# The merge's row statistics among the constants: the left side of SBUF 128 bytes higher

## The chip, the cores and the metric

The kernel runs on one core of a Trainium2 chip. Five engines share the work: TensorE (PE) multiplies matrices, VectorE (DVE) and ScalarE (ACT) do elementwise work and empty the accumulators, GpSimd (POOL) does elementwise work in SBUF, and SyncE (SP) issues most transfers. SBUF is the on-chip memory of 128 partitions; an address below is a byte within a partition. The metric is the device time of one launch in microseconds. The kernel before took 2745.03 us, the median of three runs from 2735.61 to 2746.83.

## The reference

One layer of an encoder on 2048 tokens of 1024 features, all in float32. With S = 2048 and D = 1024:

```
h  = RMSNorm(x)
z  = h @ W_in                  # (S, D) @ (D, 4352): q, k, v of two attentions, two gates
yA = windowed GQA, 8 heads, |t-s| <= 128, ALiBi and a sink logit
yB = 2-D neighbourhood attention, 8 heads, 32 x 64 grid, learned position bias
x  = x + (sigmoid(gate_A) * (yA @ Wp_A) + sigmoid(gate_B) * (yB @ Wp_B)) @ W_out
x  = x + relu(RMSNorm(x) @ W_up)^2 @ W_down      # hidden width 4096
out = RMSNorm(x)
```

## The kernel before

**Precision.** A float32 operand is split into a high and a low part in the reduced format `fp32r`; a product is three matmuls: high by high, high by low, low by high (`mm3`, lines 193 to 195, and `mm3s`, lines 239 to 241). In `PE.matmul(ps, lh, rh)` the second argument is loaded into the array as weights and the third moves through it, 512 columns at a time in most places. The result adds up in a PSUM bank.

**Stages**, in the order of time:

1. Input projection (0 to 376 us). Two of the four token blocks are multiplied by W_in with a Strassen-like scheme (`in_quad`): seven products, numbered in the order 1, 2, 5, 6, 7, 4, 3, each of 24 matmuls, or 12 where one output of 128 columns is made. The weights are `zwhl`; what moves are pages `zh1` to `zh7`. Pages 1, 2, 6, 7 and 4 lie on the left side of SBUF, pages 5 and 3 on the right.
2. Attention A (376 to 709 us) and attention B (709 to 1088 us, its last pieces to 1103). Between the attention's short matmuls stand those of a filler: the other two blocks times W_in (`feature_tile`), where `hT` moves and `whl` are the weights. In attention A `ph` and `pl` move in the product with the values, and `ka` in the scores; in attention B `phb`, `plb` and `kb`.
3. Merge (1088 to 1506 us), four token blocks. For each, eight feature tiles are made from `page` (moving) and `whl` (weights), gated, and split into `mh` and `ml`. Then four row tiles `xr` are made by 24 matmuls per bank with `mh` or `ml` as weights and `wo` moving; x is added. `rstd_of` (line 210 on) makes the row statistics: ScalarE sums the squares into `st`, VectorE adds (L218), GpSimd takes the power (L219), VectorE scales the rows (L225). The rows are turned, scaled into `h2s`, and written out.
4. Up projection (1506 to 2117 us, begun at 1447), with `ubh` moving and `uwhla`, `uwhlb` as weights, and the same seven products.
5. Down projection and the last norm (2117 to 2737 us), with `dwh` moving and `dah` as weights.

**Order of work.** Instructions stand on each engine's queue in an order that a planner writes out ahead of time. It plays the program through with estimated costs and keeps to the dependences; so the merge's `page` and `wo` matmuls, for one, are interleaved on PE. At run time each engine keeps that order and waits on semaphores.

**Memory.** Tiles come from pools. A pool with `side="left"` is stacked upward from the low end of SBUF, a pool on the right downward from the high end. The pool `cp`, opened first on the left, holds the constants and stays until the end. Sizes are rounded up to 32 bytes. Ahead of the first wide tile lie 1024 bytes for the transfers' descriptors, four framework constants of 32 bytes, and `cp`: `ident` 512, `g_mix` 32, `g_mlp` 32, `bg` 64, `sink_t` 32, `power` 32, `warm` 32. That makes 1888 = 3*512 + 352. The right side counts down from 229344 = 447*512 + 480. Wide tiles have multiples of 512 bytes, so that left tiles begin at 352 modulo 512 and right tiles at 480. There is one place on the left that differs: in the merge `mh` and `ml` are opened after `st`, whose four buffers have 32 bytes each, and so they lie 128 bytes higher, at 480. The up and down stages have all their tiles on the right.

A new tile over the place of old ones waits for their last use (`reuse_waits`), tile by tile. `T(pl, shape, dt, tag, bufs)` takes a pool, or the pool of that tag where `pl` is a dictionary; `bufs` tiles of one tag form a ring.

The pools of the merge on the left are opened in lines 922 to 925, in this order: `pwo` (for `wo`), `ph2` (for `h2s`), and the dictionary `p4x`.

Of the kernel before, what the change touches and what calls it, by code (L numbers as in the profile page):

```python
# [92 lines left out]
def encoder_layer(ctx, tc, x, norm_mix, w_in, b_gate, sink, rpb, w_pa, w_pb, w_out,  # L93
# [4 lines left out]
    def pool(name, side=None, space=None, stack=None):  # L98
        kw = {"reuse_waits": "tile"} if space is not DRAM else {}
        if side:  # L100
            kw["side"] = side
        if space:
            kw["space"] = space
        return (stack or ctx).enter_context(tc.tile_pool(name=name, bufs=1, **kw))

    def pools(stack, side, tags, name):

        return {t: pool(f"{name}_{t}", side=side, stack=stack) for t in tags}

    cp = pool("cp", side="left")  # L110
# [11 lines left out]
    def T(pl, shape, dt, tag, bufs):  # L122
        n_t[0] += 1
        pl = pl[tag] if isinstance(pl, dict) else pl
        return pl.tile(shape, dt, tag=tag, bufs=bufs, name=f"{tag}_{n_t[0]}")
# [796 lines left out]
    s_wo = ExitStack()  # L922
    pwo = pool("pwo", side="left", stack=s_wo)
    ph2 = pool("ph2", side="left", stack=s_wo)
    p4x = pools(s_wo, "left", ("xr", "junk", "st", "mh", "ml"), "m")
    wo = []

    def load_wo(n):
# [216 lines left out]
    for b in range(NB):  # L1145
        yh, yl = first_y if b == 0 else load_y(b)
        mh = T(p4x, [P, KC, BT], F32R, "mh", 1)
        ml = T(p4x, [P, KC, BT], F32R, "ml", 1)
# [261 lines left out]
```

## Time and profile before

| | |
|---|---|
| median of three runs | 2745.03 us |
| lowest, highest | 2735.61, 2746.83 us |
| the profiled execution | 2739.11 us |
| its span in the profile | 2737.3 us |
| mean granted TensorE clock | 0.989 |
| matmuls | 12332 |
| data moved by DMA | 480.86 MB, 176 GB/s on average |

In the rows that follow, PE is TensorE's matmul and PEld its weight load; "x" is a count. A group's row has line, engine, operation, tiles (written <- read), shape and count, then its busy time in us and the mean duration of one in ns, and last the idle time of the engine ahead of it and what ended that. A matmul's duration overlaps the next one's start; what a stream of matmuls costs is the spacing from start to start, which a window's length over its count gives where the engine has no idle time. "Granted clock" is the share of TensorE's full clock.

### The profile page before, as it was taken

The numbers are of one execution on the slowest core, as the hardware profiler recorded it, in microseconds if no ns is written. First come the engines' busy times: TensorE is split into PE (matmuls) and PEld (weight loads), VectorE is DVE, ScalarE is ACT, GpSimd is POOL, SyncE is SP. The second block draws the span as 40 slices with busy tenths as digits, with TensorE's granted clock in tenths as the row PEclk, the third lists the DMA queues.
The fourth block names the chain that finished last, engine by engine and source line by source line (L and its number), as shares of the span: only waits on it lengthen the run. The fifth ranks groups of instructions, "written<-read, shape, count | busy, mean of one in ns | idle before, by whom it ended". The sixth has DMA issues, their size and how long they took to land. (4 is left out here: it accounts for less than half of the span.)

```text
span 2737.3 us, 35101 instructions
## 1 busy us (share of the span) xinstructions
PE 2654.3 (97%) x12332; PEld 2185.1 (80%) x12332; DVE 1558.6 (57%) x2352; ACT 1248.0 (46%) x2225; POOL 843.0 (31%) x671
## 2 busy tenths in 40 slices
PE   7999989999899999999998999989999999999998
PEld 5888877787788888788886788878887888888887
DVE  8656446665454544634435667676664644546667
ACT  6334336665455555533433544554444232322444
POOL 1111223334455552533420366546553000000001
PEclk9999999999999999999999999999999999999999
DMA  4756384446677664745634656564434944445555
GB/s 148 199 150 197 132 245 119 115 119 176 174 210 198 177 169 144 254 142 189 202 114 166 218 199 194 184 219 147 148 136 178 325 170 162 141 158 171 180 183 175
DMA packets 329535, 480.86 MB, mean 176 GB/s; under 512 B 27896, under 2 KB 162168, under 8 KB 327184
## 3 DMA queue, kind: packets, MB, share of 16 engines
q1 hardware_dynamic: 300432, 445.06, 52.5%
q10 hardware_dynamic: 28928, 33.56, 3.8%
q8 instruction: 97, 1.59, 0.2%
q14 instruction: 78, 0.64, 0.1%
HBM read 323.28 MB, written 155.26 MB: 175 GB/s over the span
## 5 line engine op out<-in xcount | busy, mean ns | idle before, releaser
L240 PE MATMUL b<-dwh,dah 128*128 128x512 f32 x896 | 349.1, 390 | 0.0
L241 PE MATMUL b<-dwh,dah 128*128 128x512 f32 x896 | 348.2, 390 | 0.0
L239 PE MATMUL b<-dwh,dah 128*128 128x512 f32 x896 | 338.9, 390 | 1.9 <-ACT dwh L235 1.9
L232 POOL TENSOR_TENSOR uc<-uc,uc 128x512 f32<-128x512 f32 x120 | 233.6, 1961 | 208.3 <-issue 136.3
L235 ACT CAST dah<-da 128x1024 fp32r<-128x1024 f32 (+1 forms) x128 | 121.0, 945 | 365.3 <-PE b L241 240.9
L236 DVE TENSOR_TENSOR dah<-da,dah 128x1024 fp32r<-128x1024 f32 (+1 forms) x128 | 139.3, 1089 | 218.0 <-ACT dah L235 215.0
L239 PE MATMUL b<-ubh,uwhlb 128*128 128x512 f32 x592 | 232.0, 392 | 4.5 <-ACT mh L1196 2.3
L241 PE MATMUL b<-ubh,uwhlb 128*128 128x512 f32 x592 | 230.8, 392 | 3.1 <-DVE uwhlb L236 3.1
L240 PE MATMUL b<-ubh,uwhlb 128*128 128x512 f32 x592 | 231.7, 391 | 0.1
L193 PE MATMUL mm<-hT,whl 128*128 128x512 f32 x544 | 222.0, 408 | 4.5 <-DVE v L351 2.3
L195 PE MATMUL mm<-hT,whl 128*128 128x512 f32 x544 | 218.0, 401 | 1.3 <-POOL whl L176 1.3
L232 DVE TENSOR_TENSOR uc<-b,uc 128x512 f32<-128x512 f32 x160 | 108.9, 688 | 191.9 <-PE b L241 148.5
L194 PE MATMUL mm<-hT,whl 128*128 128x512 f32 x544 | 217.1, 399 | 0.0
L176 POOL TENSOR_TENSOR whl<-raw,whl 128x1024 fp32r<-128x1024 f32 x66 | 161.7, 2451 | 153.3 <-ACT whl L175 145.7
L1300 POOL TENSOR_TENSOR st<-st,power 128x1 f32<-128x1 f32 x16 | 13.6, 858 | 615.7 <-DVE st L1299 615.6
L239 PEld LDWEIGHTS b<-dwh,dah 128*128 128x128 f32 x896 | 168.4, 188 | 37.4 <-ACT dwh L235 2.3
L240 PEld LDWEIGHTS b<-dwh,dah 128*128 128x128 f32 x896 | 168.7, 188 | 35.0
L241 PEld LDWEIGHTS b<-dwh,dah 128*128 128x128 f32 x896 | 168.6, 188 | 35.0
L239 PE MATMUL zb<-zh,zwhl 128*128 128x512 f32 x476 | 189.0, 400 | 4.3 <-DVE zh L451 2.6
L240 PE MATMUL zb<-zh,zwhl 128*128 128x512 f32 x476 | 188.8, 397 | 1.8 <-DVE zh L236 1.8
L241 PE MATMUL zb<-zh,zwhl 128*128 128x512 f32 x476 | 186.9, 398 | 2.5 <-DVE zwhl L236 2.4
L239 PEld LDWEIGHTS b<-ubh,uwhlb 128*128 128x128 f32 x592 | 112.0, 189 | 28.8 <-ACT mh L1196 2.6
(242 smaller groups left out, 6229.7 us busy)
## 6 DMA issues: line engine op xcount, KB each, us to landing
at<-uc SPq DMA_DIRECT2D x224, 256.0 KB, 2.1
da<-at SPq DMA_DIRECT2D x96, 512.0 KB, 3.5
dw<-in_w_down_dram SPq DMA_DIRECT2D x160, 256.0 KB, 5.8
uraw<-in_w_up_dram SPq DMA_DIRECT2D x32, 1024.0 KB, 6.1
raw<-in_w_in_dram SPq DMA_DIRECT2D x34, 512.0 KB, 4.3
zraw<-in_w_in_dram SPq DMA_DIRECT2D x16, 1024.0 KB, 5.9
z<-zg SPq DMA_DIRECT2D x64, 256.0 KB, 2.9
xin<-in_x_dram SPq DMA_DIRECT2D x16, 512.0 KB, 6.3
```

The costliest lines, as they stand in the source:

```text
L176: G.tensor_tensor(out=hl[:, 1], in0=raw, in1=hl[:, 0].bitcast(F32), op=ALU.subtract)
L193: PE.matmul(ps, lh, rh, start=first, stop=False)
L194: PE.matmul(ps, lh, rl, start=False, stop=False)
L195: PE.matmul(ps, ll, rh, start=False, stop=last)
L232: return eng.tensor_tensor(out=out, in0=a, in1=b, op=op).ins
L235: A.copy(hi, src)
L236: eng.tensor_tensor(out=lo, in0=src, in1=hi.bitcast(F32), op=ALU.subtract)
L239: PE.matmul(ps, lh, rh, start=first, stop=False, skip_group_check=True)
L240: PE.matmul(ps, lh, rl, start=False, stop=False, skip_group_check=True)
L241: PE.matmul(ps, ll, rh, start=False, stop=last, skip_group_check=True)
L1300: G.tensor_tensor(out=r, in0=r, in1=power, op=ALU.pow)
```

## The change

The row statistics `st` of the merge no longer have a pool of their own between `junk` and `mh`; they are taken from `cp`, with the same tag, shape and ring of four. The planner sees the same instructions.

```diff
@@ -922,7 +922,9 @@
     s_wo = ExitStack()
     pwo = pool("pwo", side="left", stack=s_wo)
     ph2 = pool("ph2", side="left", stack=s_wo)
-    p4x = pools(s_wo, "left", ("xr", "junk", "st", "mh", "ml"), "m")
+    p4x = pools(s_wo, "left", ("xr", "junk", "mh", "ml"), "m")
+
+    p4x["st"] = cp
     wo = []
 
     def load_wo(n):
```

`cp` is 128 bytes larger by that for the whole kernel, so that all that lies above it on the left begins 128 bytes higher, at 2016 = 3*512 + 480: in the input projection `zh1`, `zh2`, `zh6`, `zh7`, `zh4`, `zraw` and the first two blocks' `xin`; in attention `hT`, `ka1`, `va1`, `qa`, `sa`, `ph`, `pl`, `ya`, `vb`, `sb`, `phb`, `plb`, `yb` and the small `sta`, `stb`; in the merge `wo`, `h2s`, `xr` and `junk`. `mh` and `ml` stay where they were, since 128 bytes go below `cp`'s end and 128 bytes leave their stage. Tiles on the right don't move. The kernel's tile list, written out with its pools and lifetimes, is otherwise the same.

The tiles in `st` are used in this function:

```python
        st = T(pl, [P, 4], F32, "st", 4)
        junk = T(pl if jp is None else jp, [P, 512], F32, "junk", 1)
        for n in range(2):
            A.activation(junk, t[:, n * 512 : (n + 1) * 512], AF.Square, accum_out=st[:, n : n + 1])
        r = st[:, 2 : 3]
        V.scalar_tensor_tensor(out=r, in0=st[:, 0:1], scalar=D * EPS, in1=st[:, 1:2], op0=ALU.add, op1=ALU.add)
        G.tensor_tensor(out=r, in0=r, in1=power, op=ALU.pow)
```

## The prediction

> **What bounds the kernel.** I read the page's head and its chain first, then a table of windows by stage, then stretches in which TensorE (PE) never stops, and last the waits.
>
> ```profile
> span 2737.3 us, 35101 instructions
> PE 2654.3 (97%) x12332; PEld 2185.1 (80%) x12332; DVE 1558.6 (57%) x2352; ACT 1248.0 (46%) x2225; POOL 843.0 (31%) x671
> PE 43%; DVE 1%; DMA 0%; ACT 0%; issue 0%; POOL 0%; POOLq 0%; DVEq 0%; ACTq 0%
> ```
>
> PE is busy for 97% of the span, the next engine for 57%; in the chain of what ended last the other engines have 1% between them. So the kernel ends when PE's matmuls end. The windows, with TensorE alone, show where PE has idle time (columns: stretch, its length, busy time and count, granted clock, DMA share, GB/s):
>
> ```profile
> 0.00:376.00 376.00, 358.46 (x1596) 0.99 0.57 169
> 376.00:709.00 333.00, 310.84 (x1533) 0.98 0.56 148
> 709.00:1088.00 379.00, 372.38 (x2098) 0.99 0.67 183
> 1088.00:1506.00 418.00, 401.58 (x1801) 0.99 0.53 176
> 1506.00:2117.00 611.00, 599.81 (x2622) 0.99 0.53 179
> 2117.00:2737.00 620.00, 611.20 (x2688) 0.99 0.56 187
> ```
>
> The six stages are the input projection, attention A, attention B, merge, up and down. Length less busy time is 17.5, 22.2, 6.6, 16.4, 11.2 and 8.8 us: attention A is the loosest (7%), B among the tightest (2%). The granted clock is the same nearly everywhere.
>
> **What a matmul costs, left and right.** The next table takes stretches in which PE is busy all the time, so that length over count is the spacing from one 128x512 matmul to the next. An instruction that runs in at either edge is counted, so I divide by the count less one.
>
> ```profile
> 1173.70:1207.25 33.55, 33.55 (x145) 1.00 0.19 70
> 1146.60:1156.55 9.95, 9.95 (x45) 1.00 0.70 211
> 385.51:398.98 13.47, 13.47 (x59) 1.00 0.94 250
> 2300.00:2400.00 100.00, 100.00 (x442) 1.00 0.51 167
> ```
>
> The first is wholly `pt<-wo`: 33.55/144 = 233.0 ns. The second is wholly `page`, in the same merge stage: 9.95/44 = 226.1. The third is wholly `hT`: 13.47/58 = 232.2. The fourth is the down stage: 100/441 = 226.8. All at clock 1.00, and the DMA share is lowest where the matmuls are slow, so neither clock nor traffic explains it. What moves through the array (the matmul's last operand) is on the left side in the first and third (`wo`, `hT`) and on the right in the second and fourth (`page`, `dwh`). By the pool sizes the left side begins at byte 1888 = 3*512+352 and the right side counts down from 229344 = 447*512+480. Wide tiles are whole multiples of 512, so left tiles lie at 352 and right ones at 480. The weights in all four are at 480 already: `mh` is a left tile, but `st`, 128 bytes, lies ahead of it.
>
> The input stage repeats this within one quad. Its products 1, 2, 6, 7, 4 read left pages, 5 and 3 right ones. These rows of the timeline (start, duration) begin the last 12 matmuls of product 4, the first and the fourth of 12 of product 3, and the next of product 4:
>
> ```profile
> 158.29 0.40 PE L239 MATMUL zb<-zh,zwhl 128*128 128x512 f32 x1
> ...
> 161.09 0.39 PE L239 MATMUL zb<-zh,zwhl 128*128 128x512 f32 x1
> ...
> 161.79 0.39 PE L239 MATMUL zb<-zh,zwhl 128*128 128x512 f32 x1
> ...
> 163.83 0.40 PE L239 MATMUL zb<-zh,zwhl 128*128 128x512 f32 x1
> ```
>
> The left dozen takes 2.80 us (233.3 ns each). Of the right dozen the first three still take 0.70 (233), the other nine 2.04 (226.7). Same weights ring, same stage, other page: the address decides, as far as this trace can tell.
>
> **The change, part by part.**
>
> *Which matmuls move.* These groups are counted (count, busy us, mean ns):
>
> ```profile
> L193 PE MATMUL mm<-hT,whl 128*128 128x512 f32 x544 | 222.0, 408 | 4.5 <-DVE v L351 2.3 <-ACT whl L175 2.2
> L239 PE MATMUL zb<-zh,zwhl 128*128 128x512 f32 x476 | 189.0, 400 | 4.3 <-DVE zh L451 2.6 <-DVE ze L372 0.8 <-ACT zwhl L235 0.3
> L193 PE MATMUL pt<-wo,mh 128*128 128x512 f32 x256 | 101.2, 396 | 0.4 <-ACT mh L1162 0.4
> L687 PE MATMUL av<-ph,va 128*128 128x512 f32 x92 | 38.6, 420 | 1.5 <-DVE ya L692 1.2
> L239 PE MATMUL b<-dwh,dah 128*128 128x512 f32 x896 | 338.9, 390 | 1.9 <-ACT dwh L235 1.9
> ```
>
> Each of the first three stands for three lines of equal count, the fourth for two (`ph`, `pl`). That is 1632 with `hT`, 1428 with `zh` of which 5/7 = 1020 on left pages, 768 with `wo`, 184 with `ph` and `pl`: 3604 matmuls that go from 352 to 480.
>
> *Price.* Between 352 and 480 the spacing differs by 233.0-226.8 = 6.2 ns in the merge and 232.2-226.8 = 5.4 in attention. I take 6: 3604*6 = 21.6 us. Right pages that alternate with left ones (`zh` 408, `page` 768) lose the three slow spacings after each switch, 3*6 ns in 12 matmuls or 1 ns or so for each (an estimate; `page` switches more rarely): 1.2 us. Together 22.8 us of PE time: input 1020*6+0.4 = 6.5, merge 768*6+0.8 = 5.4, attention (1632+184)*6 = 10.9. Bounds: nothing (if the address is not the cause) and 3604*6.5+2.5 = 26 (6.5 by the left dozen's 233.3).
>
> The Trainium skill ("TensorE: Matmul & The Clock Gate", section "Wait — 56ns, not 53.3ns?") gives a warm spacing of N/2.4 GHz plus about 2.5 ns, 215.7 ns at 512 columns, with no term for an address. By it the sum here would be 0. This trace has neither 215.7 nor one value: 226.8 in one place, 233.0 in another; so the sum goes by the rows.
>
> *What of it reaches the end.* Where PE does not wait, all. Where it waits for a chain that began on PE some matmuls earlier, shortening those matmuls only lengthens the wait. `hT` splits into these two windows:
>
> ```profile
> 376.00:709.00 333.00, 181.50 (x696) 0.98 0.56 148
> 709.00:1103.00 394.00, 238.07 (x936) 0.99 0.65 178
> PE s L663 <- DVE sta L665: 4.3, 7, 2.0
> PE av L688 <- DVE pl L686: 3.2, 3, 2.3
> PE s L816 <- DMA qb<-qs_b: 5.5, 2, 3.2
> ```
>
> The wait rows (total, times, longest us) are short: no chain dominates. For attention A, 696+184 matmuls or 5.3 us, I let a third be lost to such waits, since 7% of it is idle in many small pieces: 3.5. Elsewhere, 22.8-5.3 = 17.5 us, a tenth: 15.8. Sum 19.3, taken as 19 us. What is late next in attention A is the bank of scores, released by VectorE (L665).
>
> *The `st` tiles.* 128 bytes of row statistics, in a ring of four as before, now among the constants. The 16 of the merge are among these:
>
> ```profile
> L218 DVE SCALAR_TENSOR_TENSOR st<-st x32: 144/159/1909, 6.3 to 1498.8; 128x1 f32<-128x1 f32 x32
> L219 POOL TENSOR_TENSOR st<-st,power x32: 549/550/1620, 6.6 to 1499.1; 128x1 f32<-128x1 f32 x32
> ```
>
> Nothing is added: same instructions, same ring. `mh`, `ml` and everything of the up and down stages keep their addresses (`st` leaves the place ahead of `mh`, the base rises by as much). So 1231 us of 2737 have nothing to gain.
>
> *Waits by overlap.* Left and right tile edges, 128 bytes apart modulo 512 before, coincide after it. Of the pairs in which a new tile lies over an old one, a few go (`mh` over `phb`, `ubh7`, `ubh4` and `uc` over a second `wo`, `uchunk` over `h2s` or `xr`), none comes. Each such tile still lies over neighbours of equal age, so I cost this at nothing; bounds minus 2 us (one wait like `qb`, 5.5 us in 2, shorter) and 0. No DMA is added or moved in a queue.
>
> *VectorE, ScalarE.* Compare left and right:
>
> ```profile
> L235 ACT CAST zwhl<-zraw 128x1024 fp32r<-128x1024 f32 x40 | 41.7, 1049 | 68.1 <-PE zb L241 66.7 <-DVE hT L236 1.4
> L235 ACT CAST uwhlb<-uraw 128x1024 fp32r<-128x1024 f32 x52 | 54.8, 1055 | 112.7 <-PE b L241 112.7
> L686 DVE TENSOR_TENSOR pl<-pt,ph 128x512 fp32r<-128x512 f32 x92 | 62.2, 684 | 11.7 <-ACT ph L685 11.1
> L372 DVE SCALAR_TENSOR_TENSOR z<-mm,z 128x512 fp32r<-128x512 f32 x10 | 6.9, 688 | 18.2 <-ACT z L371 18.2
> ```
>
> Left sources (`zraw`, `ph`) 1049 and 684 ns, right ones (`uraw`, `z`) 1055 and 688: no gain, no loss. The B attention's narrower matmuls (`phb`, `plb`) have no right-hand twin here; 512 of them between 0 and 3 ns (half of 6, at half the width or less) are 0 to 1.5 us; I take 0.
>
> **The sum.** The profiled execution took 2739.1 us, 1.8 more than its span, and stands 5.9 under the median of the three runs, inside their spread of 11. It would become 2739.1-19 = 2720; the median becomes 2745-19 = 2726, or -0.70%, which I give as the time.
>
> **Rivals.**
> - *No change (the address isn't the cause, or not by modulo 512).* The cause would then be what goes on around the matmuls of a stage (other operands' ports, the order of products). For it: `page` and `wo` differ in more than the side, in their weights too. Against it: product 3 against 4 in one quad. Time 2745, within 3. The Trainium skill's rule above, which has no address, gives this time too; its 215.7 agrees with neither spacing here.
> - *Half is given back.* PE's shorter matmuls in all of attention, and part of the input stage, turn into waits: only the merge's 5.4 and half of the other 17.4 minus losses of 3 stay, some 11 us. Time 2734. For it: 22.2 us idle in attention A; against it: B's 2%.
> - *Slower: a new order.* The program is put in order by a planner that sees tiles and waits; with the waits above gone it may put the merge's and the up stage's work in another order, and a wait like `b` for `uwhla` arises:
>
> ```profile
> PE b L239 <- ACT uwhla L235: 5.9, 1, 5.9
> ```
>
> Once it costs 5.9; four times (once per block) 23.6, which makes 2745-19+24 = 2750. Six or more, 35 us, decide for slower by over 0.5%. Against it: the waits that go do not bind.
>
> **Chances.** Forecast (14 to 24 us saved) 0.64, half given back 0.15, no change 0.15, slower order 0.06. A run of this kernel tells some 0.5% (13.7 us) from no change. So faster by more: 0.64 and a little of the half, 0.66; within: 0.29; slower by more: 0.05. Range: the full 26 us and a median 9 lower (the lowest run, 2735.6) give 2710; at the other end half given back and part of no change, 2743.
>
> **What would show it.** The tile views have minimum, median and maximum of a matmul's duration:
>
> ```profile
> L193 PE MATMUL mm<-hT,whl x544: 390/395/776, 379.1 to 1098.8; 128*128 128x512 f32 x182
> L239 PE MATMUL b<-dwh,dah x896: 389/389/628, 2118.3 to 2728.7; 128*128 128x512 f32 x180
> ```
>
> In the profile after, stretches of `pt<-wo` and `hT` stand at 227 ns a matmul, and the median with `hT`, 395, falls to that with `dwh`, 389; input stage and merge shorter by 5 to 7 us each, attention by 6 to 11, up and down by none. The prediction is wrong if the spacing stays at 233 (another cause), or if spacing falls and PE's idle time in attention grows by as much.

## The result and the profile after

The changed kernel takes 2727.84 us (median of eight runs, 2722.83 to 2732.26) where the kernel before takes 2739.89 beside it. The ratio is 0.9953, 95% interval 0.9937 to 0.9968: 0.47% faster, 12 us by the medians, where 19 us and 0.70% were forecast. The forecast counted from 2745.03 us, the median of the first three of those eight runs before. In the two traces the instructions, their order on every engine and the semaphores that they wait for are the same; addresses alone differ. So nothing of the difference is a new order or a wait that went.

The page's head after (span, TensorE's busy time):

```profile
span 2728.7 us, 35101 instructions
PE 2638.1 (97%) x12332; PEld 2183.9 (80%) x12332; DVE 1559.3 (57%) x2352; ACT 1248.1 (46%) x2225; POOL 843.0 (31%) x671
```

PE's busy time falls from 2654.3 to 2638.1 us; that of the other engines moves by less than 1 us. Next, windows of the kernel after in which TensorE doesn't stop: left `zh` pages, `wo`, `hT`, and the down stage.

```profile
58.44:76.13 17.69, 17.69 (x79) 1.00 0.55 179
1162.39:1194.99 32.60, 32.60 (x145) 1.00 0.19 71
379.37:392.97 13.60, 13.60 (x61) 1.00 0.97 255
2300.00:2400.00 100.00, 100.00 (x442) 1.00 0.45 157
```

Length over the count less one, the spacing, is 226.8, 226.4, 226.7 and 226.8 ns. The matching stretch of `zh` in the kernel before was this:

```profile
58.02:76.40 18.38, 18.38 (x80) 1.00 0.56 172
```

That is 232.7 ns; `wo` had 233.0 and `hT` 232.2. The spacing fell where the change moved tiles and stayed at 226.8 in the down stage, as forecast. Over all matmuls that follow one another without a gap, by the start times of the two traces, the left `zh` pages go from 232.8 to 227.6 ns, `wo` from 232.9 to 227.2, but `hT` only from 232.5 to 229.3.

Where the time comes off is read from the tile views: the last number before the semicolon is the start of the last matmul of its kind. Before:

```profile
L241 PE MATMUL zb<-zh,zwhl x476: 387/392/628, 16.3 to 375.8; 128*128 128x512 f32 x159
L195 PE MATMUL mm<-hT,whl x544: 387/393/628, 381.5 to 1099.4; 128*128 128x512 f32 x182
L195 PE MATMUL pt<-wo,ml x256: 387/395/497, 1124.9 to 1492.2; 128*128 128x512 f32 x128
L241 PE MATMUL b<-ubh,uwhla x304: 388/389/632, 1449.3 to 2116.0; 128*128 128x512 f32 x152
L241 PE MATMUL b<-dwh,dah x896: 388/389/628, 2121.4 to 2729.1; 128*128 128x512 f32 x180
```

After:

```profile
L241 PE MATMUL zb<-zh,zwhl x476: 387/389/632, 16.5 to 370.2; 128*128 128x512 f32 x159
L195 PE MATMUL mm<-hT,whl x544: 387/392/793, 375.9 to 1088.7; 128*128 128x512 f32 x182
L195 PE MATMUL pt<-wo,ml x256: 387/389/501, 1113.6 to 1477.6; 128*128 128x512 f32 x128
L241 PE MATMUL b<-ubh,uwhla x304: 388/389/628, 1435.1 to 2106.9; 128*128 128x512 f32 x152
L241 PE MATMUL b<-dwh,dah x896: 388/389/393, 2113.5 to 2720.5; 128*128 128x512 f32 x180
```

The lead is 5.6 us at the end of the input stage, 10.7 after attention, 14.6 after the merge, then 9.1 after the up stage and 8.6 at the end. The up stage, whose addresses are the same in both kernels, took 5.5 us of it back in this execution. Whether that belongs to the change is one of the questions below.

The larger question is the cause. The prediction put it on the place of what moves, 352 or 480 modulo 512 ("own place" below). But in every stretch that it compared the weights lay at 480, so that the same rows fit a second theory: what counts is how far the moving tile and the weights lie apart ("relative place").

### The profile page after: what moved, and what is told of

The parts are those of the page before. It is cut to its first block, busy times and chain, and to the rows that moved or that the text cites. A ratio compares the mean times of both kernels' runs of the same rounds, so it can differ in the third digit from the quotient of the medians.

```text
span 2728.7 us, 35101 instructions
## 1 busy us (share of the span) xinstructions
PE 2638.1 (97%) x12332; PEld 2183.9 (80%) x12332; DVE 1559.3 (57%) x2352; ACT 1248.1 (46%) x2225; POOL 843.0 (31%) x671
## 4 chain that ended last, share of the span: by engine, by line
PE 85%; DMA 5%; DVE 5%; ACT 2%; issue 1%; POOL 1%; SPq 0%; ACTq 0%; POOLq 0%; DVEq 0%
PE b L239 15%; PE b L241 15%; PE b L240 15%; PE mm L195 5%; PE mm L193 5%; PE mm L194 5%; PE zb L241 4%; PE zb L240 4%; PE zb L239 4%; PE av L854 2%; PE pt L195 2%; PE pt L194 2%; PE pt L193 2%; PE s L816 2%; PE pt L843 2%
## 5 line engine op out<-in xcount | busy, mean ns | idle before, releaser
L240 PE MATMUL b<-ubh,uwhlb 128*128 128x512 f32 x592 | 232.2, 392 | 0.1
L193 PE MATMUL mm<-hT,whl 128*128 128x512 f32 x544 | 220.0, 404 | 5.1 <-DVE v L351 3.0
L195 PE MATMUL mm<-hT,whl 128*128 128x512 f32 x544 | 216.1, 398 | 1.3 <-POOL whl L176 1.3
L194 PE MATMUL mm<-hT,whl 128*128 128x512 f32 x544 | 214.6, 395 | 0.0
```

Of the source, the lines that this page charges most:

```text
L193: PE.matmul(ps, lh, rh, start=first, stop=False)
L194: PE.matmul(ps, lh, rl, start=False, stop=False)
L195: PE.matmul(ps, ll, rh, start=False, stop=last)
L240: PE.matmul(ps, lh, rl, start=False, stop=False, skip_group_check=True)
```

## The experiments

The edits shown are against the changed kernel; `...` stands for lines left out. The scratch, whose size is cut in several of them, lies at the low end of the left side, so that all tiles of that side move down by as much.

**Is it the place of what moves, or its distance from the weights?** All wide tiles were put at 352, the place that looked slow, by shifting both sides down 128 bytes.

```diff
     cp = pool("cp", side="left")
     dp = pool("dp", space=DRAM)
+    pool("rp", side="right").tile([P, 32], F32, name="pad_r")
...
-    nc = _bacc.Bacc("TRN2", target_bir_lowering=False, num_devices=1, dynamic_dma_scratch_size=1024)
+    nc = _bacc.Bacc("TRN2", target_bir_lowering=False, num_devices=1, dynamic_dma_scratch_size=896)
```

> Edit: the changed kernel, with the descriptor scratch cut by 128 bytes and a 128-byte pad ahead of the right side's first pool, so that all wide tiles of both sides, moving operands and weights alike, lie at 352 modulo 512. Same instructions in the same order. Theory 'own place' (a matmul is slow because what moves lies at 352): every 512-wide matmul spaces at 233 ns, in the up and down stages too; 5376 matmuls there by 6.2 ns are 33 us, and pages 5, 3 and page another 6: about 2740+39 = 2779 us, down stage at 233 instead of 226.7. Theory 'relative place' (a matmul is slow because what moves and its weights lie 128 bytes apart modulo 512; at the same place they don't disturb each other): 227 ns everywhere, as with all at 480: about 2728 us.

It takes 2725.23 us, ratio to before 0.9943 (0.9921 to 0.9966). The same three kinds of window, left `zh`, `wo` and the down stage:

```profile
59.67:77.17 17.50, 17.50 (x78) 1.00 0.56 181
1163.82:1196.43 32.61, 32.61 (x145) 1.00 0.20 72
2300.00:2400.00 100.00, 100.00 (x443) 1.00 0.44 150
```

227.3, 226.5 and 226.2 ns, all at 352. "Own place" foresaw 233 everywhere and 2779 us; it fails. What moves may lie at 352, if its weights do too.

A third place, 0, was tried in the same way (pad of 480 bytes, scratch of 544).

> Edit: the changed kernel with scratch cut by 480 bytes and a pad of 480 bytes on the right, so that all wide tiles of both sides lie at 0 modulo 512. 'Relative place': 227 ns everywhere, about 2728 us, as in the changed kernel. 'Own place': no row of the two kernels shows 0; if what counts is how a row of 2048 bytes lies against blocks of 512 bytes, 0 is at least as good as 480, 227 ns or less, 2728 us or less; if 480 alone were good, 233 everywhere, about 2779 us.

2725.94 us, ratio 0.9944 (0.9922 to 0.9965). Its `wo` and down windows:

```profile
1168.37:1200.97 32.60, 32.60 (x145) 1.00 0.17 60
2300.00:2400.00 100.00, 100.00 (x443) 1.00 0.45 155
```

226.4 and 226.2 ns. A start on a multiple of 512 has no merit of its own, and 226 to 227 ns is what all three common places (480, 352 and 0) give.

Then both theories in one kernel: the left side back at 352, but `mh` and `ml`, the merge's weights, with it.

```diff
-    nc = _bacc.Bacc("TRN2", target_bir_lowering=False, num_devices=1, dynamic_dma_scratch_size=1024)
+    nc = _bacc.Bacc("TRN2", target_bir_lowering=False, num_devices=1, dynamic_dma_scratch_size=896)
```

> Edit: the changed kernel with the descriptor scratch cut by 128 bytes, so that the left side is back at 352, with mh and ml, which the kernel before had at 480, at 352 too. The right side stays at 480. 'Own place': wo at 233 ns in long stretches, zh's left pages and hT at 233, as before the change; about 2740 us. 'Relative place': wo at 227 (wo and its weights mh, ml are both at 352), zh's left pages and hT at 233 (their weights are on the right, at 480); about 2735 us.

One run, 2738.42 us. Left `zh` (weights on the right, at 480) and `wo` (weights at 352):

```profile
59.32:77.46 18.14, 18.14 (x79) 1.00 0.53 174
1175.41:1208.02 32.61, 32.61 (x145) 1.00 0.18 64
```

`zh` at 232.6 ns as before the change, `wo` at 226.5 as after it. `wo` itself lies where it lay in the kernel before, at 352, where it took 233.0; its weights came to it. Here and in the other kernels that move only the left side, some instructions stand in another order, on TensorE from 1521 us on, in the up stage; the windows compared lie before that.

**The other way round: weights moved away.** In the down stage the weights `dah` were put 128 bytes off, and what moves was left at 480.

```diff
     dwh = ring(s_dn, "dwh", [P, 2, BT], F32R, 4)
+    pool("dpad", side="right", stack=s_dn).tile([P, 32], F32, name="pad_d")
     dah = ring(s_dn, "dah", [P, 2, 2, BT], F32R, 4)
```

> Edit: the changed kernel with a 128-byte pad on the right ahead of dah, so that in the down stage the weights dah lie at 352 while dwh, which moves, stays at 480. Nothing else moves but tiles of that stage. Theory 'relative place': the down stage, 2688 matmuls with next to no idle time, spaces at 233 instead of 226.7 ns: 611 us become 611+2688*6.2 = 628, the whole 2728+17 = 2745. Theory 'own place' (what moves must lie at 480): no change, 2728.

2743.51 us, ratio to before 1.0017 (1.0006 to 1.0028); against the changed kernel's 0.9953 that is 0.64% or some 17.5 us, and 17 had been worked out. The window and the last start:

```profile
2300.00:2400.00 100.00, 100.00 (x430) 1.00 0.44 149
L241 PE MATMUL b<-dwh,dah x896: 392/392/398, 2105.3 to 2730.2; 128*128 128x512 f32 x180
```

100/429 = 233.1 ns where 226.8 stood. From first to last start the row takes 624.9 us; in the changed kernel it took 607.0. In a stage in which TensorE has next to no idle time the price reaches the end in full, and it is a price on the pair of tiles: weights at 352 are slow here and were fast in all352 and left352.

**How far apart is apart?** Four kernels cut the scratch by 32, 64, 256 and 384 bytes, so that the left side lies at 448, 416, 224 and 96; the right side stays at 480.

> Edit: the changed kernel with scratch cut by 32 bytes, so that the left side lies at 448, 32 bytes off the right side's 480. wo and its weights are both at 448. If any distance between what moves and its weights costs, zh's left pages and hT (weights at 480) stand at 233 and 232.5; if a distance under 64 bytes or so is harmless, at 227.5 and 229.3 as in the changed kernel. wo at 227 either way.

> Edit: the changed kernel with scratch cut by 64 bytes: the left side at 416, 64 bytes off the right side's 480. So far distances of 32 and 128 cost some 5 ns and 256 nothing. If all but multiples of 256 cost: zh's left pages and hT at 233 and 232.5, about 2738 us; if multiples of 64 that aren't of 128 were free: 227.5 and 229.3, about 2728.

> Edit: the changed kernel with scratch cut by 256 bytes: the left side at 224, 256 bytes off the right side's 480. If places count modulo 512, zh's left pages and hT are slow, 233 and 232.5; if they count modulo 256, as fast as in the changed kernel, 227.5 and 229.3. wo at 227 either way.

> Edit: the changed kernel with scratch cut by 384 bytes: the left side at 96, which is 128 bytes above the right side's 480 modulo 512 where it was 128 below in the kernel before. If only the size of the distance counts, zh's left pages and hT stand at 233 and 232.5 as before; if its direction counts too, at another value, 227 to 240. wo at 227 either way.

One run each: 2730.45, 2736.28, 2729.51 and 2740.53 us; single runs of this kernel spread by some 10 us, so the spacing is the measure. In left448, for one, some 6 us of lead on the kernel before arise in attention, although `hT` stands there at 233.1 ns: the time of a stage varies that much from one execution to another. Left `zh` in the four kernels, in that order:

```profile
58.06:76.50 18.44, 18.44 (x80) 1.00 0.52 171
59.14:77.07 17.93, 17.93 (x78) 1.00 0.54 176
59.41:77.12 17.71, 17.71 (x79) 1.00 0.54 179
58.08:76.39 18.31, 18.31 (x80) 1.00 0.54 173
```

| left at | distance to the weights, bytes | `zh`, ns a matmul |
|---|---|---|
| 480 (the changed kernel) | 0 | 226.8 |
| 448 | -32 | 233.4 |
| 416 | -64 | 232.9 |
| 352 (the kernel before) | -128 | 232.7 |
| 224 | -256 | 227.1 |
| 96 | -384, or +128 modulo 512 | 231.8 |

A distance of 256 costs nothing, so that places count modulo 256 and not 512, as far as these six tell; 32 bytes already cost in full. `wo`, with its weights at its own place in all four, keeps to 226.5 or so.

**During which matmul?** A weight load runs beside the matmul ahead of it. In the kernel before, in the down stage, the two begin together (start, duration):

```profile
2300.07 0.39 PE L241 MATMUL b<-dwh,dah 128*128 128x512 f32 x1
2300.07 0.19 PEld L239 LDWEIGHTS b<-dwh,dah 128*128 128x128 f32 x1
```

So a misplaced weight tile could hurt while it is loaded or while it is used. The merge's triples (`mh`, `mh`, `ml`) tell these apart: on top of left352, `ml` alone went to 480.

```diff
-    p4x = pools(s_wo, "left", ("xr", "junk", "mh", "ml"), "m")
+    p4x = pools(s_wo, "left", ("xr", "junk", "mh"), "m")
+    pool("mpad", side="left", stack=s_wo).tile([P, 32], F32, name="pad_m")
+    p4x.update(pools(s_wo, "left", ("ml",), "m"))
```

> Edit: as left352 (whole left side at 352, mh and wo too), but with a pad of 128 bytes between mh and ml, so that ml alone of the merge's left tiles lies at 480. In the merge's rows the three matmuls come in the order L193 (weights mh), L194 (weights mh), L195 (weights ml), wo moving at 352. Theory 'next load' (what disturbs is the weight load of the next matmul, which runs while the present one moves its columns): L194, during which ml is loaded, spaces at over 233 ns, L193 and L195 near 227. Theory 'own weights': L195 is the slow one. Theory 'any mismatch nearby': all three at about 229 to 233. Input stage and hT as in left352, 233 and 232.5.

One run, 2737.40 us. Its timeline in a stretch of `wo`:

```profile
1174.99 0.39 PE L193 MATMUL pt<-wo,mh 128*128 128x512 f32 x1
1175.21 0.40 PE L194 MATMUL pt<-wo,mh 128*128 128x512 f32 x1
1175.45 0.40 PE L195 MATMUL pt<-wo,ml 128*128 128x512 f32 x1
1175.68 0.39 PE L193 MATMUL pt<-wo,mh 128*128 128x512 f32 x1
1175.91 0.40 PE L194 MATMUL pt<-wo,mh 128*128 128x512 f32 x1
1176.14 0.40 PE L195 MATMUL pt<-wo,ml 128*128 128x512 f32 x1
1176.37 0.39 PE L193 MATMUL pt<-wo,mh 128*128 128x512 f32 x1
```

From start to next start: L193 0.22 and 0.23, L194 0.24 and 0.23, L195 0.23 and 0.23. Over all `wo` matmuls without a gap, L193 has 227.4 ns, L194 232.2, L195 234.1. So neither simple theory holds: one misplaced load in three slows two spacings, the one in which `ml` is loaded and the one in which it is used (and the next `mh` loaded), and leaves the third. For L194 both of its own tiles lie at 352, and only the weights loaded beside it don't: 232.2 ns. That the reads of weights and moving columns get in each other's way would fit; how, these runs don't show.

**Why did `hT` gain only half?** In the kernel after, `hT` matmuls that stand eight or more deep in a run of `hT` have 227.3 ns (232.6 before), those nearer to an attention matmul or a transpose 231.1 (232.5 before), and these are about half of all. The identity, which moves in the transposes, lay at 128 and so 352 bytes off; it was put at 480.

```diff
+    cp.tile([P, 48], F32, name="pad_a")
     ident = cp.tile([P, P], F32, name="ident")
...
     warm = cp.tile([P, 1], F32, name="warm")
+    cp.tile([P, 40], F32, name="pad_z")
...
-    nc = _bacc.Bacc("TRN2", target_bir_lowering=False, num_devices=1, dynamic_dma_scratch_size=1024)
+    nc = _bacc.Bacc("TRN2", target_bir_lowering=False, num_devices=1, dynamic_dma_scratch_size=672)
```

> Edit: the changed kernel with the identity matrix, which moves in all transposes, put at 480 modulo 512 instead of 128 (scratch cut by 352, pads around the constants so that the left side begins at 2016 as in the changed kernel). In the changed kernel, hT matmuls eight or more deep in a run of hT space at 227.3 ns, those nearer to another kind of matmul at 229 to 233, 229.3 on average. Theory 'other place' (what stands before was read from another place modulo 512, and that disturbs the next ones): with the identity at 480 too, hT falls to about 227.5 on average, 1632*1.8 = 3 us less, about 2725 us. Theory 'other width' (any short matmul in between disturbs the next ones, wherever it reads): hT stays at 229.3 and the time at 2728.

2724.56 us, ratio 0.9938 (0.9916 to 0.9960), not to be told from the changed kernel's 0.9953. `hT` comes to 229.0 ns from 229.3; near other kinds to 230.6 from 231.1. The place of the identity has little part in it. The input stage of this run tells more: `zh` matmuls within eight of a transpose of `xin` have 230.5 ns, deeper ones 227.0, and there the identity, `xin`, the pages and the weights all lie at 480. A change from one 512-wide kind to another costs next to nothing: in the changed kernel, far from any other matmul, `wo` and `page` have 227.3 ns within eight of a change between them and 226.8 beyond. So it is the other kind of matmul that disturbs, even with its tiles at the same place. Whether its width does it was not tried by itself; the transposes also differ in type, float32 and not fp32r.

**Is the up stage's loss part of the change?** The changed kernel was run again.

> The changed kernel as it is. Theory 'up by chance': the up stage, whose instructions and addresses are the same before and after, and which took 6.0 us longer in the first profile after, takes 625 to 628 us here as in the other kernels of this study, and the ratio to before comes out at 0.994 to 0.995. Theory 'up by the change': 632 us again.

2724.86 us in six runs beside 2739.16 of before, 0.9948 by these medians and inside the interval of the first measurement. The same rows as above for this execution:

```profile
L241 PE MATMUL zb<-zh,zwhl x476: 387/389/628, 17.1 to 370.5; 128*128 128x512 f32 x159
L195 PE MATMUL mm<-hT,whl x544: 387/392/795, 376.8 to 1091.5; 128*128 128x512 f32 x182
L195 PE MATMUL pt<-wo,ml x256: 387/389/497, 1117.0 to 1480.1; 128*128 128x512 f32 x128
L241 PE MATMUL b<-ubh,uwhla x304: 388/389/632, 1437.9 to 2105.7; 128*128 128x512 f32 x152
L241 PE MATMUL b<-dwh,dah x896: 388/389/389, 2109.9 to 2716.9; 128*128 128x512 f32 x180
```

The lead is 5.3 us after the input stage, 7.9 after attention, 12.1 after the merge, 10.3 after the up stage, 12.2 at the end. In the first execution after, a wait for VectorE in the up stage was longer; the rows are of before, after, and after again (us in total, times, longest):

```profile
PE b L239 <- DVE uc L232: 5.4, 2, 4.5
PE b L239 <- DVE uc L232: 10.5, 2, 6.0
PE b L239 <- DVE uc L232: 6.2, 2, 4.5
```

5.1 of the 5.5 us were this wait, and it did not come again. That it comes and goes from one execution to the next is shown; why is not.

## Why the prediction came out as it did

**What bounds the kernel** was right: most of what the spacing saved in the input stage and the merge came off these stages (the numbers follow under the price), and down_apart's 17 us, put on a stage with next to no idle time, arrived whole. The chain with which the prediction argued could not show this for the changed stages: PE's 43% and the others' 1% are 44% of the span, so it reaches back over the up and down stages alone.

**What a matmul costs, left and right.** The sizes were read rightly (226.8 against 233) and the sum went the right way. The step of the mechanism that failed is "the address decides": the rows compared moving tiles at 352 and 480, but all with weights at 480, which the prediction noted and did not use. It is the distance, modulo 256 by the places tried. For this change both readings give the same number, since it brings the left side to the place of the right, and that is luck; for all352 they differ by 50 us, and own place was wrong by all of it.

**The price.** Input: 6.5 us of PE time forecast, 5.9 by the spacings (1020 by 5.3 ns and 408 by 1.3); 5.6 and 5.3 us came off in two executions, where nine tenths, 5.9, were expected. Merge: 5.4 forecast, 4.7 by the spacings (768 by 5.7 and 768 by 0.4), 3.9 and 4.2 came off. Attention: 10.9 forecast, 5.3 by the spacings (1632 by 3.2, `ph` and `pl` next to nothing). This is the term that was mis-sized. The 6 ns came from a long run of `hT`, and within attention they hold in such runs alone; among the short matmuls a 512-wide one has 231.1 ns after the change and had 232.5 before it.

**What of it reaches the end.** Of attention's 5.3 us, 5.1 came off in one execution and 2.6 in the other, so that the loss to waits can't be told from what executions differ by. Forecast were 8.5. Up and down stages were put at nothing, which holds in addresses and spacing. Of the stages' gains named as signs, 5 to 7 us for input and merge and 6 to 11 for attention, only the input stage's came true in both executions.

**The rivals.** "No change" fails on the windows, which have 226 to 227 ns after and 232 to 233 before. With it fails the Trainium skill's rule without an address ("TensorE: Matmul & The Clock Gate", section "Wait — 56ns, not 53.3ns?"; 215.7 ns): the runs have neither that nor one value. "Half is given back", 11 us, came near in size, for another reason: the gain in attention was never there to give back. "A new order" did not come: order and waits are the same in both traces. The Trainium skill ("SBUF — State Buffer", section "Who interferes with whom") gives TensorE two SBUF read ports, one for the moving operand and one for weight loads, and calls them independent. The runs here differ on that as far as time goes: between the kernel before and left352 in `wo`, and between the changed kernel and down_apart in the down stage, the weights alone have another place, and the spacing changes by 6 ns; in ml480, L194 is slowed by a load alone.

**The number.** The forecast of 2726 us lies within 2 us of the measured 2727.84, and part of that is luck: the base of three runs stood 5 us above the median of eight, which hid that the saving was 12 us and not 19. These 12 lie below the 14 to 24 to which 0.64 was given. The 0.47% is just inside the bound of 0.5%, with the interval on both sides of it, so the result fell to "within", at 0.29, and not to "faster by more", at 0.66.

## What to carry to other kernels

In a kernel bound by matmuls it is worth a try to put moving tiles and weights at the same place modulo 256 bytes: in this one's streams of 512-wide fp32r matmuls, each with a weight load, it gave 6 ns in 233, for 128 bytes put elsewhere and no instruction. When two groups of rows differ in one property, write down what else they have in common before calling that property the cause; here one kernel with everything at the "bad" place settled it. A spacing read in a long uniform run isn't the spacing of the same matmul among short ones of another kind.

## What the runs showed of the hardware that was not expected

- The spacing of 512-wide fp32r matmuls depends on the distance between the moving tile and the weights: 226.8 ns at 0 and 227.1 at 256 bytes, 231.8 to 233.4 at 32, 64 and 128. The place of either by itself made no difference (480, 352 and 0).
- A single misplaced weight tile in three slows two spacings, 232.2 and 234.1 against 227.4.
- After a matmul of another kind (the attention's, or a transpose) the spacing of 512-wide ones takes about ten of them to settle, even with all tiles at one place: with `hT` after the change 231.1 ns over the first eight, 228.1 for the tenth, 226.8 for the eleventh.
